# A gated delta-net stage: key chain rearranged, value pairs convolved from a copied slot, inverse's products four ticks later

## The chip, the cores and the metric

The kernel runs on one core of one Trainium2 chip. The metric is the device time of one execution in microseconds (us). Engines are named as in the profile: PE is TensorE (matmuls; PEld its weight loads), DVE is VectorE, ACT is ScalarE, POOL is GpSimd, SP is SyncE, whose queue issues the loads. SBUF is the core's main on-chip memory; PSUM holds the banks into which PE writes.

## What is computed

The reference is a trunk of two layers over 256 tokens of width 1024 (float32). Each layer is a feed-forward block, a mixer and a second feed-forward block, with RMS norms around each. The mixer of layer 0 is a short gated convolution; that of layer 1 is a gated delta-net, and the change lies in it alone. Cut to what matters:

```python
qkv = silu(causal_depthwise_conv(qkv, conv_w))          # width 4, on q, k and v
q = repeat(l2norm(q)); k = repeat(l2norm(k))            # 8 key heads for 16 value heads
beta = sigmoid(b)
g = -exp(a_log) * softplus(a + dt_bias)
# per head, in chunks of tokens:
a = strict(einsum(k_beta, k) * decay)
t_inv = triangular_solve(eye + a, eye)
u = t_inv @ v_beta; w = t_inv @ (k_beta * exp(g))
qk = causal(einsum(q, k) * decay)
# scan over chunks:
v_new = u - w @ state
o = (q * exp(g)) @ state + qk @ v_new
state = state * exp(g_last) + k_tail.T @ v_new
# out:
o = rms_norm(o) * norm_w * silu(z); y = o @ w_out
```

`l2norm(x)` is `x * rsqrt(sum(x * x) + EPS)`.

## The kernel before

The 256 tokens are two tiles of 128 (`NT` = 2, index t). A weight arrives as float32 by a DMA into a buffer `raw`, ACT rounds it to `whi` (L119) and DVE forms the rest `wlo` (L121, called a weight split below); each product of the reference is three matmuls (x with whi, the rest of x with whi, x with wlo). The heads are worked on in four groups (`NG` = 4, gi) of four value heads and two key heads (kh).

The function `gdn_proj` runs the products of the delta-net's input projection in this order: the first heads of queries and keys, the other queries and keys (`stat_group`, 24 products of 256 columns each, L278 to L280), the gate z of three groups (L221 to L225), the values of four groups, and the last z. The output projection follows (L323 to L325). Beside this main line run side chains, written as Python generators. A `Ticker` counts a tick for every twelve products of `stat_group`; `yield n` hands the program back to the main line for n ticks, so the numbers of ticks fix where in the program, and so where in each engine's queue, a side chain's step stands. Each engine works off its queue in that order and waits at an instruction until what it needs is there.

The side chains that matter here:

- `kq_chain` (L605): for each key head, PE transposes key and query into a bank `tp` (L618) and multiplies keys with keys and queries into a bank `pk` (L621). ACT copies the transposed key out (`ktok`, L624), copies the second token tile (`kq1`, L625), and takes four squares with a running sum (`junk`, L630), key and query of each token tile. At the end of a group, POOL adds EPS to the eight sums (L634), DVE takes the reciprocal (L636), POOL multiplies by beta (`dsc`, L639), and DVE scales the products by that and the decays (`KQ`, L645, eight steps). ACT copies the diagonal blocks of 32 x 32 into one tile (`blk`, L652, eight copies a group). POOL also forms `nk`, `eq` and `wt` for later use.
- `invert` (L667): it starts when `kq_chain` ends. DVE transposes the tile (L669), solves 31 steps (L677, L679), and transposes the inverse twice, into `Xd` (L681) and `Yd` (L683). POOL copies Yd's blocks into KQ (L689, 32 copies). `INV_WAIT` = 37 ticks after the start, in two halves, POOL fills blocks E from Xd (L699) and PE and ACT build the inverse of 128 x 128 from the blocks (L707 to L742).
- `v_pair` (L748): for two value heads, `conv` scales the bank on ACT (L584) and adds three taps on DVE for each head (L586), from the PSUM bank that the products were written to; silu follows on ACT (L573); `V_WAIT` = 4 ticks later PE transposes the result (L757) and ACT scales it out (`nv`, L759).
- `scan` waits for a group's values and inverse and then solves, updates the state and forms the outputs (L771 to L837); `z_chain` scales them with z (L846 to L855).

The banks that the side chains take come from a pool of four (`acc`), those of the main products and of the values' transposes from another of four (`mm`). Slots for tiles of 128 x 512 float32 come from one pool of 22 (`slab`); there are three buffers `raw`.

Of the kernel before, what the change touches and what calls it, by code (L numbers as in the profile page):

```python
# [7 lines left out]
F32 = mybir.dt.float32  # L8
F32R = mybir.dt.float32r
AF = mybir.ActivationFunctionType  # L10
ALU = mybir.AluOpType
PSUM = bass.MemoryType.PSUM

P = 128
T = 256
NT = 2
# [5 lines left out]
NG = 4  # L22
B32 = 32
EPS = 1e-6
# [6 lines left out]
NBIG = 8  # L31
NROW = 3
KQ_WAIT = 3
INV_WAIT = 37
V_WAIT = 4
SCAN_WAIT = 2
ORD = "00111222"
GORD = "00012222"
# [11 lines left out]
def trunk_kernel(ctx: ExitStack, tc: tile.TileContext, x, norm_g, w_gu, w_dn, sc_in, sc_cw, sc_out,  # L50
                 gdn_h0, gdn_h1, gdn_a0, gdn_a1, gdn_a2, gdn_v, gdn_z, gdn_cw, gdn_al, gdn_dt, gdn_nw, gdn_out, eye, upper, slower, out, stop=None):
    nc = tc.nc
    V, S, G, PE = nc.vector, nc.scalar, nc.gpsimd, nc.tensor
# [6 lines left out]
    sp = ctx.enter_context(tc.tile_pool(name="sp", bufs=2))  # L60
# [16 lines left out]
    phalf = const.tile([P, 4], F32, name="phalf")  # L77
# [49 lines left out]
    def slab(shape, dtype, name):  # L127
        return hp.tile(shape, dtype, name=name, tag="slab")
# [347 lines left out]
    def gdn_proj(xh, xl, mid):  # L476
# [102 lines left out]
        KQ = [[None] * NT for _ in range(NG)]  # L579
# [25 lines left out]
        def kq_chain():  # L605

            for gi in range(NG):
                ss = sp.tile([P, NT, 2, 2], F32, name="kss", bufs=2)
                k1 = slab([P, 2, 2, P], F32, "kq1")
                pkq = []  # L610
                for i in range(2):
                    kh = 2 * gi + i
                    while kq[kh] is None or tk.now < kq_time[kh] + KQ_WAIT:
                        yield 1
                    tp = side_bank().rearrange("p (t c) d -> p t c d", t=NT)
                    for t in range(NT):
                        for c in range(2):
                            PE.transpose(tp[:, t, c, :], kq[kh][:, c, t * P:(t + 1) * P], ident)  # L618
                    pk = side_bank().rearrange("p (t c) d -> p t c d", t=NT)
                    for t in range(NT):  # L620
                        PE.matmul(pk[:, t, :, :], lhsT=kq[kh][:, 0, t * P:(t + 1) * P],  # L621
                                  rhs=kq[kh][:, :, t * P:(t + 1) * P], start=True, stop=True)
                    pkq.append(pk)
                    S.activation(ktok[:, kh, :], tp[:, 0, 0, :], AF.Copy)  # L624
                    S.activation(k1[:, i, :, :], kq[kh][:, :, P:], AF.Copy)  # L625
                    kq1[kh] = k1[:, i, :, :]
                    for t in range(NT):
                        for c in range(2):
                            junk = sp.tile([P, 512], mybir.dt.bfloat16, name="junk", bufs=1)
                            S.activation(junk[:, 0:P], tp[:, t, c, :], AF.Square, accum_out=ss[:, t, c, i:i + 1])  # L630
                    yield 1
                while dec[1][gi] is None:
                    yield 1
                G.tensor_scalar(ss, ss, EPS, None, ALU.add)  # L634
                rk = sp.tile([P, NT, 2], F32, name="rk", bufs=2)
                V.reciprocal(rk, ss[:, :, 0, :])  # L636
                dd = small(f"dsc{gi}", 8).rearrange("p (t n) -> p t n", t=NT)
                for t in range(NT):
                    G.tensor_tensor(dd[:, t, :].rearrange("p (k v) -> p k v", k=2),  # L639
                                    beta[:, t, 4 * gi:4 * gi + 4].rearrange("p (k v) -> p k v", k=2),  # L640
                                    rk[:, t, :].unsqueeze(2).broadcast_to([P, 2, 2]), ALU.mult)
                for t in range(NT):
                    m = big([P, 4, 2, P], F32, "KQ")
                    for hv in range(4):
                        V.scalar_tensor_tensor(m[:, hv, :, :], pkq[hv // 2][:, t, :, :], dd[:, t, hv:hv + 1],  # L645
                                               bc(dec[t][gi][:, hv, :], 2), ALU.mult, ALU.mult)
                    KQ[gi][t] = m
                    for b in range(4):
                        r = slice(b * B32, (b + 1) * B32)
                        o = Ld[r, :, 8 * gi + t:8 * gi + t + 7:2].rearrange("p i v -> p v i")  # L650
                        i_ = m[r, :, 0, b * B32:(b + 1) * B32]
                        S.activation(o, i_, AF.Copy)  # L652
                n = small(f"nk{gi}", 4).rearrange("p (t n) -> p t n", t=NT)
                G.tensor_tensor(n, ss[:, :, 0, :], phalf.rearrange("p (t n) -> p t n", t=NT), ALU.pow)
                q = small(f"eq{gi}", 4).rearrange("p (t n) -> p t n", t=NT)
                G.tensor_scalar(q, ss[:, :, 1, :], 128.0 * EPS, None, ALU.mult)
                w = small(f"wt{gi}", 4)
                G.tensor_tensor(w, etail[:, 4 * gi:4 * gi + 4], dd[:, 0, :], ALU.mult)
                Dsc[gi], nk[gi], eq[gi], wt[gi] = dd, n, q, w
                yield 1  # L660
            tk.start(invert())


# [3 lines left out]
        def invert():  # L667
# [5 lines left out]
            for j in range(B32 - 1):  # L673
                n, m = B32 - 1 - j, j + 1
# [7 lines left out]
            Yd = row("blk").rearrange("p (a b) -> p a b", a=B32)  # L682
            V.transpose(Yd.rearrange("p h i -> p i h"), X)  # L683
            T1 = row("blk").rearrange("p (a b) -> p a b", a=B32)
            for gi in range(NG):
                for t in range(NT):
                    for b in range(4):
                        r = slice(b * B32, (b + 1) * B32)
                        G.tensor_copy(KQ[gi][t][r, :, 0, r], Yd[r, 8 * gi + t:8 * gi + t + 7:2, :])  # L689
            yield INV_WAIT  # L690
            for half in range(2):
                hs = slice(16 * half, 16 * half + 16)
                gis = (2 * half, 2 * half + 1)
                E = {}
                for gi in gis:
                    E[gi] = slab([P, 8, 64], F32, "E64")
                    for b in range(2):
                        r = slice(b * B32, (b + 1) * B32)
                        G.tensor_copy(E[gi][r, :, r], Xd[r, 8 * gi:8 * gi + 8, :])  # L699
                    G.memset(E[gi][0:B32, :, B32:], 0.0)  # L700
                pt = side_bank().rearrange("p a (b c) -> p (a b) c", c=B32)
                for x in range(16):
                    ht = 16 * half + x
# [42 lines left out]
        nv = [None] * NG  # L746

        def v_pair(gi, i, pt, tiles):  # L748
            vc = sp.tile([P, 2, T], F32, name="yb")
            for j in range(2):  # L750
                conv(vc[:, j, :], pt[:, j, :], 16 + 4 * gi + 2 * i + j)
            silu(vc, vc)
            yield V_WAIT
            tp = ps.tile([P, NT, 2, P], F32, name="mm")
            for t in range(NT):
                for j in range(2):
                    PE.transpose(tp[:, t, j, :], vc[:, j, t * P:(t + 1) * P], ident)  # L757
            for t in range(NT):
                S.activation(tiles[t][:, 2 * i:2 * i + 2, :], tp[:, t, :, :], AF.Copy,  # L759
                             scale=nk[gi][:, t, i:i + 1])  # L760
            if i == 1:
                nv[gi] = tiles
# [293 lines left out]
```

## Time and profile before

| what | us |
|---|---|
| median of three runs | 1131.45 (1130.69 to 1131.48) |
| profiled execution, its own time | 1128.42 |
| its span, from first to last instruction | 1126.5 |
| PE, DVE, ACT, POOL busy | 1100.2, 749.9, 651.8, 88.8 |
| mean granted TensorE clock | 0.995 |

A row of the timeline gives the start in the span, the duration, engine, line, operation, output and inputs by the program's names, the shape and the count; in brackets how long the engine stood idle before it and what it had waited for. Rows of groups give busy time and the mean in ns of one, then idle time before them. The view of one line gives the shortest, median and longest in ns. Names of buffers are given without their numbers.

### The profile page before, as it was taken

The numbers are of one execution on the slowest core, as the hardware profiler recorded it, in microseconds if no ns is written. First come the engines' busy times: TensorE is split into PE (matmuls) and PEld (weight loads), VectorE is DVE, ScalarE is ACT, GpSimd is POOL, SyncE is SP. The second block draws the span as 40 slices with busy tenths as digits, with TensorE's granted clock in tenths as the row PEclk, the third lists the DMA queues.
The fourth block names the chain that finished last, engine by engine and source line by source line (L and its number), as shares of the span: only waits on it lengthen the run. The fifth ranks groups of instructions, "written<-read, shape, count | busy, mean of one in ns | idle before, by whom it ended". The sixth has DMA issues, their size and how long they took to land.

```text
span 1126.5 us, 16842 instructions
## 1 busy us (share of the span) xinstructions
PE 1100.2 (98%) x6284; PEld 942.4 (84%) x6284; DVE 749.9 (67%) x1140; ACT 651.8 (58%) x1201; POOL 88.8 (8%) x167
## 2 busy tenths in 40 slices
PE   9999999999999999999999999889899999999997
PEld 6888887888788888788888877778899887888886
DVE  7776735687777663577765468768946557767543
ACT  6666535545556653556664358784587645666432
POOL 0100000000200000010000012110141212000000
PEclk9999999999999999999999999999999999999999
DMA  8755555656566565576555653327332355655552
GB/s 271 244 185 190 191 166 167 225 180 198 182 223 204 171 206 165 163 229 209 189 185 169 193 185 113 94 94 227 114 129 76 131 168 168 213 199 190 185 168 75
DMA packets 55955, 198.12 MB, mean 176 GB/s; under 512 B 6721, under 2 KB 7233, under 8 KB 55874
## 3 DMA queue, kind: packets, MB, share of 16 engines
q1 hardware_dynamic: 55728, 196.99, 54.2%
q8 instruction: 49, 0.80, 0.3%
q14 instruction: 32, 0.26, 0.1%
q10 hardware_dynamic: 146, 0.07, 0.0%
HBM read 195.99 MB, written 1.05 MB: 175 GB/s over the span
## 4 chain that ended last, share of the span: by engine, by line
PE 81%; DVE 7%; ACT 5%; DMA 3%; issue 2%; POOL 2%; SPq 0%; DVEq 0%; POOLq 0%; ACTq 0%
PE mm L298 27%; PE mm L301 14%; PE acc L324 7%; PE acc L325 7%; PE acc L323 7%; PE mm L221 3%; PE mm L222 3%; PE mm L225 3%; DVE wlo L121 2%; ACT whi L119 1%; ACT blk L652 1%; DVE kq L586 1%; PE mm L176 1%; ACT junk L147 1%; DMA raw<-in_w_gu 1%
## 5 line engine op out<-in xcount | busy, mean ns | idle before, releaser
L121 DVE TENSOR_TENSOR wlo<-raw,whi 128x1024 fp32r<-128x1024 f32 (+2 forms) x362 | 437.5, 1220 | 240.2 <-ACT whi L119 201.5
L119 ACT ACTIVATE whi<-raw 128x1024 fp32r<-128x1024 f32 (+2 forms) x362 | 376.1, 1051 | 224.3 <-PE acc L325 104.6
L298 PE MATMUL mm<-x,whi 128*128 128x512 f32 x1312 | 329.4, 393 | 0.0
L298 PEld LDWEIGHTS mm<-x,whi 128*128 128x128 f32 x1312 | 235.9, 189 | 42.4
L301 PEld LDWEIGHTS mm<-x,wlo 128*128 128x128 f32 x1312 | 179.0, 190 | 12.8
L301 PE MATMUL mm<-x,wlo 128*128 128x256 f32 x1312 | 182.9, 282 | 0.0
L323 PE MATMUL acc<-whi,hb 128*128 128x512 f32 x352 | 136.5, 388 | 0.0
L324 PE MATMUL acc<-wlo,hb 128*128 128x512 f32 x352 | 135.6, 385 | 0.3 <-DVE wlo L121 0.3
L325 PE MATMUL acc<-whi,hb 128*128 128x512 f32 x352 | 135.3, 385 | 0.0
L308 ACT ACTIVATE corr<-mm 128x256 f32<-128x256 f32 x164 | 61.2, 376 | 67.4 <-PE mm L301 65.6
L221 PE MATMUL mm<-whi,x 128*128 128x512 f32 (+1 forms) x240 | 94.4, 394 | 0.9 <-ACT x L178 0.7
L222 PE MATMUL mm<-wlo,x 128*128 128x512 f32 (+1 forms) x240 | 94.2, 393 | 0.7 <-DVE wlo L121 0.7
L225 PE MATMUL mm<-whi,x 128*128 128x512 f32 (+1 forms) x240 | 87.8, 389 | 0.2 <-DVE x L179 0.2
L324 PEld LDWEIGHTS acc<-wlo,hb 128*128 128x128 f32 x352 | 66.2, 188 | 13.8 <-DVE wlo L121 0.8
L323 PEld LDWEIGHTS acc<-whi,hb 128*128 128x128 f32 x352 | 66.2, 188 | 13.1
L325 PEld LDWEIGHTS acc<-whi,hb 128*128 128x128 f32 x352 | 66.1, 188 | 13.2
L154 POOL TENSOR_SCALAR rstd<-ss 128x1 f32<-128x1 f32 x24 | 12.3, 513 | 786.1 <-ACT junk L147 786.1
L278 PE MATMUL mm<-x,whi 128*128 128x256 f32 x200 | 59.7, 299 | 2.0 <-DVE kq L586 2.0
L279 PE MATMUL mm<-x,whi 128*128 128x256 f32 x200 | 58.4, 292 | 0.0
L280 PE MATMUL mm<-x,wlo 128*128 128x256 f32 x200 | 57.9, 289 | 0.0
L222 PEld LDWEIGHTS mm<-wlo,x 128*128 128x128 f32 x240 | 45.2, 188 | 11.2 <-DVE wlo L121 2.9
L221 PEld LDWEIGHTS mm<-whi,x 128*128 128x128 f32 x240 | 45.2, 188 | 11.1 <-ACT x L178 2.7
(216 smaller groups left out, 1238.3 us busy)
## 6 DMA issues: line engine op xcount, KB each, us to landing
raw<-in_w_gu SPq DMA_DIRECT2D x176, 512.0 KB, 4.2
raw<-in_w_dn SPq DMA_DIRECT2D x88, 512.0 KB, 3.6
raw<-in_sc_in SPq DMA_DIRECT2D x24, 512.0 KB, 4.1
raw<-in_gdn_z SPq DMA_DIRECT2D x16, 512.0 KB, 3.9
raw<-in_gdn_v SPq DMA_DIRECT2D x16, 512.0 KB, 4.2
raw<-in_gdn_out SPq DMA_DIRECT2D x16, 512.0 KB, 3.7
gamma<-in_norm_g SPq DMA_DIRECT2D x11, 512.0 KB, 5.4
raw<-in_gdn_a SPq DMA_DIRECT2D x9, 512.0 KB, 4.4
```

What stands on the lines that cost most here:

```text
L119: S.activation(hi[:, r], raw[:, r], AF.Copy)
L121: newest[0] = V.tensor_tensor(lo[:, r], raw[:, r], hi[:, r], ALU.subtract).ins
L221: PE.matmul(pt, lhsT=xh[:, t, k, :], rhs=hi, start=(k == 0), stop=False)
L222: PE.matmul(pt, lhsT=xh[:, t, k, :], rhs=lo, start=False, stop=False)
L225: PE.matmul(pt, lhsT=xl[:, t, j, :], rhs=part(j)[0], start=False, stop=(j == KD - 1))
L278: PE.matmul(ptile, lhsT=hi, rhs=h2, start=(k == 0), stop=False)
L298: PE.matmul(flat, lhsT=part(k, 0), rhs=xx[:, k].rearrange("p h t q -> p (h t q)"), start=(k == 0), stop=False)
L301: PE.matmul(flat[:, T:], lhsT=part(k, 1), rhs=xx[:, k, 0].rearrange("p t q -> p (t q)"), start=False, stop=(k == KD - 1))
L308: S.activation(c, pt[:, 1, :], AF.Copy)
L323: PE.matmul(o, lhsT=yh(c, t), rhs=hi[:, r], start=(c == 0), stop=False)
L324: PE.matmul(o, lhsT=yh(c, t), rhs=lo[:, r], start=False, stop=False)
L325: i = PE.matmul(o, lhsT=yl(c, t), rhs=hi[:, r], start=False, stop=(c == n - 1)).ins
```

## The change

`INV_WAIT` goes from 37 to 41 and `V_WAIT` becomes one number per group, (8, 8, 4, 4). In `kq_chain` the key squares come first, and all four squares stand ahead of the copies of `ktok` and `kq1`; the addition of EPS for the keys and `dsc` move from POOL to DVE, the addition for the queries becomes part of `eq`; and half of the diagonal copies move from ACT to POOL. In `invert` POOL's copies of Yd into KQ move behind the blocks E, in two halves. In `v_pair` the first two groups copy the bank to a slot (`vraw`) on ACT, and the conv reads that. After the change line numbers are one to nine higher.

```diff
-INV_WAIT = 37
-V_WAIT = 4
+INV_WAIT = 41
+V_WAIT = (8, 8, 4, 4)
+VRAW = 2
...
-                ss = sp.tile([P, NT, 2, 2], F32, name="kss", bufs=2)
+                ss = sp.tile([P, 2, NT, 2], F32, name="kss", bufs=2)
...
+                    for c in range(2):
+                        for t in range(NT):
+                            junk = sp.tile([P, 512], mybir.dt.bfloat16, name="junk", bufs=1)
+                            S.activation(junk[:, 0:P], tp[:, t, c, :], AF.Square, accum_out=ss[:, c, t, i:i + 1])
                     S.activation(ktok[:, kh, :], tp[:, 0, 0, :], AF.Copy)
                     S.activation(k1[:, i, :, :], kq[kh][:, :, P:], AF.Copy)
                     kq1[kh] = k1[:, i, :, :]
-                    for t in range(NT):
-                        for c in range(2):
-                            junk = sp.tile([P, 512], mybir.dt.bfloat16, name="junk", bufs=1)
-                            S.activation(junk[:, 0:P], tp[:, t, c, :], AF.Square, accum_out=ss[:, t, c, i:i + 1])
...
-                G.tensor_scalar(ss, ss, EPS, None, ALU.add)
+                V.tensor_scalar(ss[:, 0], ss[:, 0], EPS, None, ALU.add)
...
-                    G.tensor_tensor(dd[:, t, :].rearrange("p (k v) -> p k v", k=2),
+                    V.tensor_tensor(dd[:, t, :].rearrange("p (k v) -> p k v", k=2),
...
-                        S.activation(o, i_, AF.Copy)
+                        if b < 2:
+                            S.activation(o, i_, AF.Copy)
+                        else:
+                            G.tensor_copy(o, i_)
...
-                G.tensor_scalar(q, ss[:, :, 1, :], 128.0 * EPS, None, ALU.mult)
+                G.tensor_scalar(q, ss[:, 1], EPS, 128.0 * EPS, ALU.add, ALU.mult)
...
-            for gi in range(NG):
-                for t in range(NT):
-                    for b in range(4):
-                        r = slice(b * B32, (b + 1) * B32)
-                        G.tensor_copy(KQ[gi][t][r, :, 0, r], Yd[r, 8 * gi + t:8 * gi + t + 7:2, :])
             yield INV_WAIT
...
-                    G.memset(E[gi][0:B32, :, B32:], 0.0)
+                    placed = G.memset(E[gi][0:B32, :, B32:], 0.0).ins
+                for gi in gis:
+                    for t in range(NT):
+                        for b in range(4):
+                            r = slice(b * B32, (b + 1) * B32)
+                            with tc.issue_after(placed):
+                                G.tensor_copy(KQ[gi][t][r, :, 0, r], Yd[r, 8 * gi + t:8 * gi + t + 7:2, :])
...
+            if gi < VRAW:
+                raw = slab([P, 2, T], F32, "vraw")
+                S.activation(raw, pt, AF.Copy)
+                pt = raw
             vc = sp.tile([P, 2, T], F32, name="yb")
...
-            yield V_WAIT
+            yield V_WAIT[gi]
```

On DVE, at the end of the first group's keys, before (`kq` is a query or key under its conv, `rk` the reciprocal, `acc` the banks of products):

```order
L586 SCALAR_TENSOR_TENSOR kq_6753<-mm_6677,gcw_6224,kq_6753 128x255
L636 RECIPROCAL rk_6826<-kss_6549 128x4
L586 SCALAR_TENSOR_TENSOR kq_6753<-mm_6782,gcw_6224,kq_6753 128x255
L586 SCALAR_TENSOR_TENSOR kq_6753<-mm_6677,gcw_6224,kq_6753 128x254
L645 SCALAR_TENSOR_TENSOR KQ_6831<-acc_6740,dsc0_6828,dec_6622 128x256
L586 SCALAR_TENSOR_TENSOR kq_6753<-mm_6677,gcw_6224,kq_6753 128x253
L645 SCALAR_TENSOR_TENSOR KQ_6831<-acc_6740,dsc0_6828,dec_6622 128x256
```

And the same place after:

```order
L635 TENSOR_SCALAR kss_6549<-kss_6549 128x4
L637 RECIPROCAL rk_6826<-kss_6549 128x4
L640 TENSOR_TENSOR dsc0_6828<-beta_6233,rk_6826 128x4 x2
L646 SCALAR_TENSOR_TENSOR KQ_6831<-acc_6740,dsc0_6828,dec_6622 128x256 x2
L646 SCALAR_TENSOR_TENSOR KQ_6840<-acc_6740,dsc0_6828,dec_6627 128x256 x2
L646 SCALAR_TENSOR_TENSOR KQ_6831<-acc_6800,dsc0_6828,dec_6622 128x256
L587 SCALAR_TENSOR_TENSOR kq_6753<-mm_6677,gcw_6224,kq_6753 128x255
```

The two small steps of POOL now stand on DVE around the reciprocal, and the first five KQ steps stand ahead of the next key's conv taps.

On DVE, around the end of the inverse, before (`yb_7803` is the third value pair, `yb_7895` the fourth; `blk_7350` is Xd, `blk_7352` is Yd):

```order
L586 SCALAR_TENSOR_TENSOR yb_7803<-mm_7717,gcw_6224,yb_7803 128x253
L677 TENSOR_TENSOR sg_7344<-blk_7252,blk_7254 128x60
L121 TENSOR_TENSOR wlo_7870<-raw_7867,whi_7869 128x1024
L679 TENSOR_TENSOR blk_7254<-blk_7254,sg_7344 128x2x30
L586 SCALAR_TENSOR_TENSOR yb_7895<-mm_7783,gcw_6224,yb_7895 128x255
L677 TENSOR_TENSOR sg_7347<-blk_7252,blk_7254 128x31
L121 TENSOR_TENSOR wlo_8276<-raw_8273,whi_8275 128x1024
L679 TENSOR_TENSOR blk_7254<-blk_7254,sg_7347 128x31
L586 SCALAR_TENSOR_TENSOR yb_7895<-mm_7783,gcw_6224,yb_7895 128x254
L681 STREAM_TRANSPOSE blk_7350<-blk_7254 128x32x32
L683 STREAM_TRANSPOSE blk_7352<-blk_7254 128x32x32
L586 SCALAR_TENSOR_TENSOR yb_7895<-mm_7783,gcw_6224,yb_7895 128x253
```

After (`yb_7770` is the third value pair, `yb_7864` the fourth):

```order
L587 SCALAR_TENSOR_TENSOR yb_7770<-vraw_7768,gcw_6224,yb_7770 128x253
L681 TENSOR_TENSOR sg_7347<-blk_7252,blk_7254 128x31
L587 SCALAR_TENSOR_TENSOR yb_7770<-vraw_7768,gcw_6224,yb_7770 128x255
L683 TENSOR_TENSOR blk_7254<-blk_7254,sg_7347 128x31
L122 TENSOR_TENSOR wlo_8097<-raw_8094,whi_8096 128x1024
L685 STREAM_TRANSPOSE blk_7350<-blk_7254 128x32x32
L687 STREAM_TRANSPOSE blk_7352<-blk_7254 128x32x32
L587 SCALAR_TENSOR_TENSOR yb_7770<-vraw_7768,gcw_6224,yb_7770 128x254
L587 SCALAR_TENSOR_TENSOR yb_7864<-vraw_7862,gcw_6224,yb_7864 128x255
L587 SCALAR_TENSOR_TENSOR yb_7770<-vraw_7768,gcw_6224,yb_7770 128x253
```

Before, the third pair's last tap stood ahead of both transposes; now its last two taps stand behind them. On PE the third pair's transposes stand ahead of the inverse's first product in both kernels, 25 rows ahead of it.

On POOL, where the inverse's blocks are filled, before (`E64` are the blocks E):

```order
L699 COPY E64_7929<-blk_7350 32x8x32 x2
L699 COPY E64_7933<-blk_7350 32x8x32 x2
L700 MEMSET E64_7933 32x8x32
L699 COPY E64_8127<-blk_7350 32x8x32
L689 COPY KQ_6831<-blk_7352 32x4x32 x4
L689 COPY KQ_6840<-blk_7352 32x4x32 x4
L689 COPY KQ_6946<-blk_7352 32x4x32 x4
L689 COPY KQ_6955<-blk_7352 32x4x32 x4
L689 COPY KQ_7055<-blk_7352 32x4x32 x4
```

After:

```order
L698 COPY E64_7968<-blk_7350 32x8x32 x2
L699 MEMSET E64_7968 32x8x32
L705 COPY KQ_6831<-blk_7352 32x4x32 x4
L705 COPY KQ_6840<-blk_7352 32x4x32 x4
L705 COPY KQ_6946<-blk_7352 32x4x32 x4
L705 COPY KQ_6955<-blk_7352 32x4x32 x4
L698 COPY E64_8211<-blk_7350 32x8x32 x2
L699 MEMSET E64_8211 32x8x32
L698 COPY E64_8215<-blk_7350 32x8x32 x2
```

The second half's blocks E now stand behind sixteen of the copies into KQ, where before all but one of their steps stood behind all thirty-two.

On SP, two of the sixteen loads of the output weights move ahead of the two gamma loads (ten ahead and six behind, where it was eight and eight).

More of the change, by code (lines that the diff above doesn't have):

```diff
@@ L633, in kq_chain @@
                     yield 1
-                G.tensor_scalar(ss, ss, EPS, None, ALU.add)
+                V.tensor_scalar(ss[:, 0], ss[:, 0], EPS, None, ALU.add)
                 rk = sp.tile([P, NT, 2], F32, name="rk", bufs=2)
-                V.reciprocal(rk, ss[:, :, 0, :])
+                V.reciprocal(rk, ss[:, 0])
                 dd = small(f"dsc{gi}", 8).rearrange("p (t n) -> p t n", t=NT)
                 for t in range(NT):
-                    G.tensor_tensor(dd[:, t, :].rearrange("p (k v) -> p k v", k=2),
+                    V.tensor_tensor(dd[:, t, :].rearrange("p (k v) -> p k v", k=2),
                                     beta[:, t, 4 * gi:4 * gi + 4].rearrange("p (k v) -> p k v", k=2),
@@ L651, in kq_chain @@
                         i_ = m[r, :, 0, b * B32:(b + 1) * B32]
-                        S.activation(o, i_, AF.Copy)
+                        if b < 2:
+                            S.activation(o, i_, AF.Copy)
+                        else:
+                            G.tensor_copy(o, i_)
                 n = small(f"nk{gi}", 4).rearrange("p (t n) -> p t n", t=NT)
-                G.tensor_tensor(n, ss[:, :, 0, :], phalf.rearrange("p (t n) -> p t n", t=NT), ALU.pow)
+                G.tensor_tensor(n, ss[:, 0], phalf.rearrange("p (t n) -> p t n", t=NT), ALU.pow)
                 q = small(f"eq{gi}", 4).rearrange("p (t n) -> p t n", t=NT)
-                G.tensor_scalar(q, ss[:, :, 1, :], 128.0 * EPS, None, ALU.mult)
+                G.tensor_scalar(q, ss[:, 1], EPS, 128.0 * EPS, ALU.add, ALU.mult)
                 w = small(f"wt{gi}", 4)
```

## The prediction

> **What bounds the kernel now.** I began with the first part of the page, the busy time of each engine.
>
> ```profile
> PE 1100.2 (98%) x6284; PEld 942.4 (84%) x6284; DVE 749.9 (67%) x1140; ACT 651.8 (58%) x1201; POOL 88.8 (8%) x167
> ```
>
> TensorE (PE) is busy 98% of the span, so the kernel is bound by its matmuls, and the change adds and removes none. All that can change is the 26 us in which PE stands, and the time in which it runs slowly. Second I read the windows of ten microseconds through the stage that the diff touches. The columns are the window, PE, PEld, DVE, ACT and POOL busy with their instruction counts, the granted clock, the DMA share and GB/s.
>
> ```profile
> 720.00:730.00 10.00, 9.46 (x73) 8.70 (x72) 6.88 (x17) 9.54 (x35) 2.05 (x6) 1.00 0.11 42
> 730.00:740.00 10.00, 7.75 (x52) 6.94 (x51) 8.43 (x21) 8.79 (x24) 2.04 (x6) 1.00 0.29 106
> 740.00:750.00 10.00, 6.94 (x26) 5.48 (x25) 6.08 (x11) 8.55 (x30) 0.25 (x2) 0.83 0.36 110
> 790.00:800.00 10.00, 6.59 (x44) 6.39 (x43) 9.97 (x26) 6.57 (x10) 0.00 (x0) 0.83 0.22 63
> ```
>
> Two places lose time: 720 to 750, the key chain, where ScalarE (ACT) is the fullest helper, and 790 to 800, the first value heads, where VectorE (DVE) has no idle time at all. In both the granted clock falls to 0.83 in the worst window. Third I read who PE waits for between 715 and 835 us (total, times, longest).
>
> ```profile
> PE acc L618 <- ACT kq L573: 3.6, 2, 3.1
> PE mm L757 <- ACT yb L573: 3.4, 1, 3.4
> PE acc L621 <- DVE KQ L645: 1.7, 1, 1.7
> PE acc L618 <- ACT junk L630: 0.5, 2, 0.4
> PE acc L718 <- ACT blk L711: 0.4, 1, 0.4
> PE acc L707 <- DVE blk L681: 0.2, 1, 0.2
> ```
>
> The first, third and fourth rows are the key chain: 3.6 + 1.7 + 0.5 = 5.8 us. The second is the first value pair. The last two are the inverse's products. Last, the timeline of PE at the longest wait, which shows that a wait costs more than itself.
>
> ```profile
> 794.53 1.12 PE L757 MATMUL mm<-ident,yb 128*128 128x128 f32 x4 [3.41 <-ACT yb L573]
> ...
> 797.57 0.37 PE L279 MATMUL mm<-x,whi 128*128 128x256 f32 x1
> 797.78 0.28 PE L280 MATMUL mm<-x,wlo 128*128 128x256 f32 x1
> 797.90 0.28 PE L278 MATMUL mm<-x,whi 128*128 128x256 f32 x1
> ```
>
> Equal products start 0.21 us apart until 797.78 and 0.12 apart from then on. The slow spell lasts about 3.2 us from the restart, and 3.2 x (1 - 0.12/0.21) = 1.4 us is lost in it. The key chain's longest wait fills the other window of clock 0.83 (740 to 750, 3.06 us without PE), so I charge it the same 1.4; the 1.7 us wait lies in a window of clock 1.00, and nothing is charged. [...]
>
> **The key chain.** The chain per group was, in the rows of the first group on POOL and DVE:
>
> ```profile
> 717.26 0.66 POOL L634 TENSOR_SCALAR kss<-kss 128x8 f32<-128x8 f32 x1 [14.02 <-ACT junk L630]
> 718.00 1.05 POOL L654 TENSOR_TENSOR nk<-kss,phalf 128x4 f32<-128x4 f32 x1
> ...
> 719.45 0.35 POOL L639 TENSOR_TENSOR dsc<-beta,rk 128x4 f32<-128x4 f32 x2
> ...
> 719.68 0.48 DVE L645 SCALAR_TENSOR_TENSOR KQ<-acc,dsc,dec 128x256 f32<-128x256 f32 x1 [0.63 <-POOL dsc L639]
> ```
>
> From the first POOL step to the first KQ are 2.4 us, and nk, which the KQ step doesn't need, stands ahead of dsc for 1.05 of them. Now the addition, reciprocal and two dsc run on DVE; small DVE steps aren't all in this trace, and four of 0.2 us (POOL's dsc pair takes 0.35) make 0.8. That saves about 1.6 us a group. The key squares go to the front of ACT's list, where they pass two copies and four query squares. KQ then comes earlier, and the waits for KQ and for junk should go (2.2 us). What's late next is the silu of the queries, behind ACT's list. That list gets shorter by 16 of these 32 copies; this row prices a copy on ACT, and POOL's copies of the same shape (a row under the rivals) have a median of 0.29.
>
> ```profile
> L652 ACT ACTIVATE blk<-KQ 32x128 f32<-32x128 f32 x32 | 13.8, 430 | 2.3 <-DVE KQ L645 2.0
> ```
>
> So 16 x 0.43 = 6.9 us leave ACT and 16 x 0.29 = 4.6 go to POOL, which was 20% busy in these windows. Walking PE, ACT and DVE through the new order with these durations, I find the wait of 3.06 us down to 0.45, without a slow spell, and one new wait of 1.0 us for the keys' transposed copy (ktok), which now stands behind the four squares. Gain by the rows: 5.8 + 1.4 - 0.45 - 1.0 = 5.8 us. The same walk, read at the end of the last key product, gives 7.9, since a wait also delays the restart. I take 6.5; the bounds are 3.5 (two of the small margins of 0.1 to 0.3 us in the walk fail and cost another 2.3) and 8. The z products behind the key chain get no wait in the walk. The inverse, which starts when the last group's copies end, moves from 758.0 to about 749: 7.9 us from the chain, and about 1.1 because the last copies run on two engines.
>
> **The value pairs.** The first row is the first value product on PE; the second is the first pair's silu, which came late because its conv did, on a full DVE:
>
> ```profile
> 778.01 0.28 PE L278 MATMUL mm<-x,whi 128*128 128x256 f32 x1
> ...
> 793.84 0.63 ACT L573 ACTIVATE yb<-yb 128x512 f32<-128x512 f32 x1 [0.23 <-DVE yb L586]
> ```
>
> A tick is 12 products, 12 x 0.12 = 1.44 us. Before, the first transposes were due nine ticks in, at 778.0 + 13.0 = 791.0; they began at 794.53. Now they are due after 13 ticks, and the walk has the first product at 769.7: 769.7 + 18.7 = 788.4. Each next pair comes four ticks and its forerunner's transposes (0.44) later: 794.6 and 800.8. Conv and silu of the first two pairs end at 784.2 and 791.4 in the walk. So the wait of 3.4 goes with its slow spell: +4.8 us, with 3 to 4 us of cover left. The four bank copies cost ACT 4 x 0.63 = 2.5 us (the silu row has their shape), on an engine that has 3.4 us idle in the window of 790 to 800; they lie ahead of the conv, and that cover holds them.
>
> The inverse's products also move 4 ticks, and its 0.5 us of waits go, since its transposes end at about 800.2 and the products are due at 800.8 + 0.44 + 24 x 0.12 = 804.1. If that cover is gone it costs 0.2 to 0.5 again.
>
> **The new wait.** The third pair is the cost. Before, its conv was through before the inverse's two transposes of DVE; these rows are the inverse's first step, its two transposes, a tap of the fourth pair behind them, and the weight splits of 760 to 812:
>
> ```profile
> 758.02 1.25 DVE L669 STREAM_TRANSPOSE blk<-blk 128x1024 f32<-128x1024 f32 x1 [2.01 <-ACT blk L652]
> ...
> 809.80 2.20 DVE L681 STREAM_TRANSPOSE blk<-blk 128x1024 f32<-128x1024 f32 x1
> 811.89 1.96 DVE L683 STREAM_TRANSPOSE blk<-blk 128x1024 f32<-128x1024 f32 x1
> 813.69 0.41 DVE L586 SCALAR_TENSOR_TENSOR yb<-mm,gcw,yb 128x253 f32<-128x253 f32 x1
> ...
> L121 DVE TENSOR_TENSOR wlo<-raw,whi 128x1024 fp32r<-128x1024 f32 x18 | 21.9, 1217 | 2.0 <-ACT whi L119 1.7
> ```
>
> In the new order the last two of its six taps stand behind both transposes, with a tap of the fourth pair between. The inverse took 813.8 - 758.0 = 55.8 us on DVE from its first transposition to its last. One weight split (1.2) and four taps (4 x 0.41 = 1.6) fewer stand within now, so from 749 it ends at about 802.0. Three taps (1.2) and the silu (0.6) end at 803.8, while PE wants the pair at 800.8. (If the key chain yields less, both sides move together.) Waiting PE has the rest of the fifth pair's products and the inverse's products queued behind, and the scan follows those. That is 3.0 us; I take 2.9 and the slow spell of 1.4: -4.3. From below it costs almost nothing (the 2.0 us that DVE stood before splits close up, and the copies leave DVE sooner); from above 4.5 + 1.4 and 0.5 at the fifth pair, whose conv follows on DVE: -6.4.
>
> Behind this the order is the old one up to a block of products; the scan is 4 ticks later, its gamma loads two loads later. I put that at 0, with 1.5 either way. **Sum:** 6.5 + 4.8 + 0.5 - 4.3 = 7.5 us. The profiled run took 1128.42 us with a span of 1126.5, 1.9 outside it, and lies 3.0 under the median of 1131.45. I take the gain off the median: 1123.9 us.
>
> **Rivals.** *No third wait.* If DVE closes its gaps, the gain is 6.5 + 4.8 + 0.5 = 11.8: 1119.6. For it: the idle time of DVE. Against: the order, which holds whatever the speed.
>
> *The key chain hardly gains.* ACT was 95% busy from 720 to 730; if the queries' silu stays late and ktok's wait brings a slow spell, the key term is 2 and the gain 3.0: 1128.4.
>
> *POOL locked out (slower).* The value taps now read two SBUF tensors, and POOL copies 32 blocks beside them. This case shows what that does: taps out of SBUF beside POOL's selects, taps out of a bank, and POOL's copies beside weight splits.
>
> ```profile
> L586 DVE SCALAR_TENSOR_TENSOR kq<-mm,gcw,kq x27: 463/473/484, 705.4 to 743.6; 128x255 f32<-128x255 f32 x9, 128x254 f32<-128x254 f32 x9, 128x253 f32<-128x253 f32 x9
> L586 DVE SCALAR_TENSOR_TENSOR kq<-craw,gcw,kq x21: 472/475/861, 690.3 to 706.6; 128x255 f32<-128x255 f32 x7, 128x254 f32<-128x254 f32 x7, 128x253 f32<-128x253 f32 x7
> ...
> 812.07 1.72 POOL L699 COPY E<-blk 32x256 f32<-32x256 f32 x4 [58.84 <-DVE blk L681]
> ...
> L689 POOL COPY KQ<-blk x32: 283/287/1190, 815.4 to 827.6; 32x128 f32<-32x128 f32 x32
> ```
>
> A tap out of a bank never takes over 484 ns; out of SBUF it takes up to 861, and a copy up to 1190 instead of 287. The blocks E of a half are four copies, 1.72, and two memsets, by estimate from these copies 0.3 each: 2.3 us. So the copies begin at 800.2 + 2.3 = 802.5, and with the second half's E between, the last ends at 805 + 32 m for a mean of m each. PE wants it at 819.7 + 4.3 = 824. At the median of 0.29 they end at 814; from m = 0.59 PE waits, from m = 0.83 the gain of 7.5 is gone, and at 1.0, 837, the change is slower by 5.5: 1137. For it: three splits and seven taps fall beside the first half. Against: before, two of 32 copies were long. [...]
>
> **Chances.** The forecast 0.55 (own range 1121 to 1127), no third wait 0.23, key chain hardly gains 0.15, POOL locked out 0.07. The range of 1117 to 1130.5 takes in the upper bound of the key term on the good side (14 us of gain) and the lower bounds together on the other (3.5 + 4.8 + 0.5 - 6.4 - 1.5 = 0.9). A measurement of this kernel tells 0.2%, 2.3 us, from no change. The first two cases and a third of the third are faster by more: 0.83. Same: 0.10. Slower: 0.07.
>
> **What would show it.** Right: PE's waits for KQ and junk gone, the last wait for the queries under 1 us, the first value pair's wait gone, a new wait of about 3 us at the third value pair's transposes that ends with a silu behind the two transposes on DVE, and the inverse begun 8 to 9 us earlier. Wrong: more than 2 us of waits left from 720 to 750; no wait at the third pair; waits for POOL's copies in the inverse's last products; or new waits in the scan above 1.5 us.

## The result and the profile after

| kernel | median of 7 runs, us | lowest to highest |
|---|---|---|
| before | 1131.44 | 1130.69 to 1131.64 |
| after | 1123.13 | 1121.73 to 1129.65 |

The ratio is 0.9942, with a 95% interval of 0.9921 to 0.9962. That is 6.6 us by the ratio and 8.3 us by the medians, where 7.5 were forecast. The profiled execution of the changed kernel took 1122.99 us, its span was 1121.3.

The two profiles don't enter the stage at the same time, so all that follows is counted from the first transposes of keys on PE (704.00 before, 706.12 after). Three marks divide the stage: the first value product, the inverse's first step on DVE, and the start of the last three products of the output projection.

| from the first key transposes, us | before | after | forecast of the gain |
|---|---|---|---|
| inverse begins | 54.0 | 46.4 | 8 to 9 |
| first value product ("key part") | 74.0 | 66.5 | 6.5 (walk: 7.9) |
| from there to the stage's end ("value part") | 155.3 | 155.5 | 1.0 |

So the key part gave 7.5 us and the value part lost 0.2. Who PE waits for after 715 us, in the changed kernel (total, times, longest):

```profile
PE mm L766 <- ACT yb L574: 2.5, 1, 2.5
...
PE acc L622 <- ACT ktok L629: 1.0, 1, 1.0
PE acc L737 <- ACT E L727: 0.8, 1, 0.8
...
PE acc L723 <- ACT blk L716: 0.4, 1, 0.4
```

The rows for KQ, for the last query's silu and for the first value pair are gone. The wait of 1.0 for `ktok` is the one that was forecast, and the 2.5 is the third value pair. This is its chain: first the two last transposes of the inverse on DVE and the taps behind them, then the silu on ACT, then PE:

```profile
800.33 2.23 DVE L685 STREAM_TRANSPOSE blk<-blk 128x1024 f32<-128x1024 f32 x1
802.43 2.05 DVE L687 STREAM_TRANSPOSE blk<-blk 128x1024 f32<-128x1024 f32 x1
804.30 3.07 DVE L587 SCALAR_TENSOR_TENSOR yb<-vraw,gcw,yb 128x254 f32<-128x254 f32 x7
...
805.70 0.63 ACT L574 ACTIVATE yb<-yb 128x512 f32<-128x512 f32 x1 [0.75 <-DVE yb L587]
...
806.38 1.11 PE L766 MATMUL mm<-ident,yb 128*128 128x128 f32 x4 [2.45 <-ACT yb L574]
```

And POOL's copies of the inverse's blocks into KQ, 16 and 16, with what stands between:

```profile
805.40 9.59 POOL L705 COPY KQ<-blk 32x128 f32<-32x128 f32 x16
815.05 0.83 POOL L698 COPY E<-blk 32x256 f32<-32x256 f32 x2
...
816.28 2.74 POOL L698 COPY E<-blk 32x256 f32<-32x256 f32 x2
...
819.44 5.30 POOL L705 COPY KQ<-blk 32x128 f32<-32x128 f32 x16
```

The first half took 9.59 / 16 = 0.60 us a copy. Copy by copy, the six beside a tap out of a slot took 0.36 to 0.41 us, the four beside a weight split 1.17 to 1.31, and the other six, beside taps out of a bank or between DVE's steps, 0.29 or 0.30. The second half, beside a DVE that had no work but two taps out of a bank at its end, took 5.30 / 16 = 0.33 with the time between the copies. Over all 32 the mean is (9.59 + 5.30) / 32 = 0.47, under the 0.59 from which the prediction would have had PE wait, and PE didn't wait for them. The two copies into E at 815.05 stood beside taps out of a bank; those at 816.28 stood beside two weight splits and took more than three times as long.

The clock, in the windows of ten microseconds, is 0.83 in two places:

```profile
710.00:720.00 10.00, 10.00 (x71) 9.89 (x70) 8.12 (x20) 7.55 (x29) 1.41 (x4) 0.83 0.33 107
720.00:730.00 10.00, 9.03 (x66) 8.32 (x65) 8.37 (x20) 9.26 (x37) 3.93 (x7) 1.00 0.41 118
730.00:740.00 10.00, 10.00 (x73) 9.46 (x72) 9.37 (x25) 9.71 (x29) 5.66 (x9) 1.00 0.45 140
740.00:750.00 10.00, 10.00 (x47) 8.07 (x46) 8.88 (x21) 8.30 (x24) 3.86 (x7) 1.00 0.50 153
...
800.00:810.00 10.00, 7.55 (x51) 7.35 (x51) 10.00 (x13) 5.28 (x10) 6.79 (x14) 0.83 0.21 59
```

From 730 to 750 PE is full now, where it was busy 7.75 and 6.94. The largest loss sits at 800 to 810.

### The profile page after: what moved, and what is told of

Its sections match the earlier page's. It is cut to its first block, busy times and chain, and to the rows that moved or that the text cites. A ratio compares the mean times of both kernels' runs of the same rounds, so it can differ in the third digit from the quotient of the medians.

```text
span 1121.3 us, 16866 instructions
## 1 busy us (share of the span) xinstructions
PE 1100.0 (98%) x6284; PEld 942.7 (84%) x6284; DVE 753.1 (67%) x1152; ACT 647.5 (58%) x1189; POOL 98.1 (9%) x171
## 3 DMA queue, kind: packets, MB, share of 16 engines
q1 hardware_dynamic: 55728, 196.99, 53.9%
## 5 line engine op out<-in xcount | busy, mean ns | idle before, releaser
L120 ACT ACTIVATE whi<-raw 128x1024 fp32r<-128x1024 f32 (+2 forms) x362 | 376.2, 1051 | 228.8 <-PE acc L326 104.1
L325 PEld LDWEIGHTS acc<-wlo,hb 128*128 128x128 f32 x352 | 66.2, 188 | 13.7 <-DVE wlo L122 0.8
L324 PEld LDWEIGHTS acc<-whi,hb 128*128 128x128 f32 x352 | 66.2, 188 | 13.4 <-ACT hb L473 0.2
L279 PE MATMUL mm<-x,whi 128*128 128x256 f32 x200 | 59.6, 298 | 2.0 <-DVE kq L587 2.0
```

The lines of the kernel that those rows point to most:

```text
L120: S.activation(hi[:, r], raw[:, r], AF.Copy)
L279: PE.matmul(ptile, lhsT=hi, rhs=h2, start=(k == 0), stop=False)
L324: PE.matmul(o, lhsT=yh(c, t), rhs=hi[:, r], start=(c == 0), stop=False)
L325: PE.matmul(o, lhsT=yh(c, t), rhs=lo[:, r], start=False, stop=False)
```

## The experiments

Theory to test, as the prediction had it: the parts add up, 6.5 us from the key chain and 1.0 from the rest. Each ratio is to the kernel before on the same chip. "Key chain alone" is the kernel before with the whole new `kq_chain` (squares first, small steps on DVE, half of the copies on POOL) and nothing else.

**One part each.** `e1_key_only` is the key chain alone.

> The key chain's part alone, on the kernel before. The prediction's theory: the parts are independent, and the key chain is worth 6 to 7.5 us; the first value pair keeps its wait of about 3.4 us with its slow spell. Time 1124 to 1125.5, ratio about 0.994. Rival (the key chain hardly gains, the gain came with the value pairs): 1 to 3 us, ratio 0.997 to 0.999.

Measured: 1120.17 us against 1130.74, ratio 0.9909 (0.9891 to 0.9928). The key chain alone gives more than the whole change: its five runs (1118.96 to 1121.18) all lie under the changed kernel's seven (from 1121.73) and its six of a later repetition (from 1121.74). PE's waits and the first value pair in it:

```profile
PE mm L760 <- ACT yb L573: 1.9, 2, 1.6
PE acc L621 <- ACT ktok L628: 1.0, 1, 1.0
...
786.37 0.66 PE L760 MATMUL mm<-ident,yb 128*128 128x128 f32 x4 [1.58 <-ACT yb L573]
```

With four ticks and no slots, the wait of 3.41 us has become 1.58, without a slow spell behind it. The inverse leads the first value product by 20.1 us, as before (20.0). But from its first step to about the pair's silu DVE does 13 weight splits where it did 14, and stands 1.0 us before them where it stood 2.0 (these rows are of before, 758 to 794 us, and of the key chain alone, 751.5 to 787):

```profile
L121 DVE TENSOR_TENSOR wlo<-raw,whi 128x1024 fp32r<-128x1024 f32 x14 | 17.0, 1218 | 2.0 <-ACT whi L119 1.7
```

```profile
L121 DVE TENSOR_TENSOR wlo<-raw,whi 128x1024 fp32r<-128x1024 f32 x13 | 15.8, 1218 | 1.0 <-ACT whi L119 1.0
```

That makes 2.2 us, and the pair's wait is 1.8 shorter. The parts don't add: what the later transposes were to remove, the key chain had mostly removed.

`e2_value_only` is the changed kernel with the old `kq_chain`.

> All of the change but the key chain's part. The prediction's theory: the first pair's 4.8 us and 0.5 us at the inverse go, a wait of 2.5 to 3 us with a slow spell of 1.4 comes at the third value pair: gain 1 to 1.5 us, ratio about 0.999. Rival (no third wait without the earlier inverse): gain 5 us, ratio 0.9955. Rival (the key chain hardly gains, so this part carries the 8 us): ratio 0.993 to 0.994.

Measured: 1137.18, ratio 1.0061 (1.0040 to 1.0083): slower, which no theory had. Its waits:

```profile
PE mm L763 <- ACT yb L574: 3.9, 1, 3.9
...
PE acc L720 <- ACT blk L713: 1.6, 2, 1.2
PE mm L223 <- DVE wlo L122: 1.2, 1, 1.2
```

The first pair's wait is gone, the third pair's is 3.9, and two more follow. From the first value product on, the waits are 7.4 us where before had 4.1, and behind them PE loses 6.8 us to a slower clock where before lost 1.7.

**The third pair's wait.** `e3_third_first` is the changed kernel with

```diff
+            yield INV_TR
             Xd = row("blk").rearrange("p (a b) -> p a b", a=B32)
             V.transpose(Xd.rearrange("p h c -> p c h"), X.rearrange("p i c -> p c i"))
...
-            yield INV_WAIT
+            yield INV_WAIT - INV_TR
```

and `INV_TR = 33`, which puts five of the third pair's taps ahead of the first transpose and the sixth between the two.

> The changed kernel with the inverse's two last transposes created 33 ticks later, so that five taps of the third value pair stand ahead of the first of them and the sixth ahead of the second. The prediction's theory: the third pair's wait of 2.5 us falls to 0.3 or less and its slow spell of about 1.4 goes, nothing takes its place: 3.5 to 4 us less than the changed kernel, about 1119.3, ratio 0.9907. Rival (VectorE is the bound of this stretch, so that the wait moves to the fifth pair and to the blocks E of the inverse): at most 1 us less, ratio 0.9935.

Measured: 1122.97, ratio 0.9935 (0.9917 to 0.9953), as the rival had it. The third pair no longer waits, and the inverse's next step does:

```profile
811.82 0.47 ACT L586 ACTIVATE yb<-mm,gcw 128x256 f32<-128x256 f32 x1 [1.16 <-DVE yb L588]
812.32 1.20 ACT L718 ACTIVATE blk<-acc 32x512 f32<-32x512 f32 x2
...
812.96 0.31 PE L725 MATMUL acc<-blk 32*32 32x32 f32 x2 [3.59 <-ACT blk L718]
```

The copy that PE waits for stands on ACT behind a scaling that waits for DVE's taps. DVE was busy 9.90 and 10.00 of 10 us in the windows 790 to 800 and 800 to 810, so here a step moved ahead of another only changed who waits.

`e4_no_vraw` is the changed kernel with `VRAW = 0`.

> The changed kernel without the copies from bank to slot: all convs read the bank, all waits as changed. Theory that the copies only cost ScalarE 2.5 us that is hidden: within 1 us of the changed kernel, the third pair's wait stays at 2 to 3 us. Rival (the slots are what lets the transposes come eight ticks later, since a bank held until the conv's end makes the products wait): new waits of TensorE for a bank behind a conv, 2 us or more, ratio 0.996 or worse.

Measured: 1121.26, ratio 0.9927 (0.9907 to 0.9948), no different from the changed kernel's. The slots bring nothing that can be told. Without them the third pair's wait is gone (its last tap stands ahead of the transposes), a wait of 0.9 for a bank comes (L279 behind `nv`), and 2.2 at the inverse's second step (L723).

**Which edit costs.** `f1_key_vals` is the key chain alone with the new `v_pair`; `f2_key_inv` is it with the new `invert` and 41 ticks.

> The key chain's part with the change to the value pairs (8, 8, 4, 4 ticks and the slots), the inverse as before. Theory: with the key chain alone the first pair's wait is down to 1.6 us, so the later transposes have 1.9 us to win, and VectorE's two long transposes take it back: a wait of about 1.3 us at the inverse's first product and about 1 at the third pair; 1119.5 to 1121, ratio 0.990 to 0.9915. Rival (the later transposes and slots alone cost the 3 us that lie between the key chain alone and the whole change): 1123, ratio 0.9935.

> The key chain's part with the change to the inverse (41 ticks, POOL's copies behind the blocks E), the value pairs as before. Theory: nothing waits for the inverse in the kernel with the key chain alone, so four ticks more bring nothing, and they cost nothing as the scan has work beside it: within 1 us of it, ratio 0.990 to 0.992. Rival (the scan four ticks later lays its serial steps open near the end, or POOL's locked copies are late for the last products): 2 to 3 us more, ratio 0.993 to 0.9935.

Measured: 1120.64 us, ratio 0.9932 (0.9910 to 0.9954), and 1122.60 us, ratio 0.9936 (0.9922 to 0.9951). `f2_key_inv` lies nearer to its rival, 3 us above the key chain alone. `f1_key_vals` is not decided: its median lies in the theory's range, but two of its nine runs took 1126.2 and 1128.4, and by the ratio it lies with the rival. Both intervals overlap with that of the key chain alone. Of the two waits that the theory of `f1_key_vals` named, the one at the inverse's first product is there (1.5); the other came at the inverse's second step (1.7) and not at the third pair. In `f2_key_inv` the scan's L784 waits 1.2 us for DVE and a block E 0.6.

**What in the key chain it is.** From the key chain alone, one edit undone each: all copies to `blk` on ACT (`f3_key_actblk`), EPS and `dsc` on POOL (`g1_key_poolsmall`), the four squares behind the two copies and in the old order (`g2_key_oldsq`).

```diff
-                        if b < 2:
-                            S.activation(o, i_, AF.Copy)
-                        else:
-                            G.tensor_copy(o, i_)
+                        S.activation(o, i_, AF.Copy)
```

> The key chain's part with all 32 diagonal copies on ScalarE as before. Theory: the 6.9 us that left ScalarE's list are what made the last query's silu early: its wait of 2.5 to 3 us with the slow spell of 1.4 comes back, and the inverse starts 1 us later: 4 to 5 us more than the key chain alone, 1124.5, ratio 0.995. Rival (the gain is in the short chain from squares to KQ alone): less than 1.5 us more, ratio 0.992 or better.

Measured: 1127.91, ratio 0.9981 (0.9969 to 0.9993), 8 us of the 10 lost. The theory's wait came back (3.5), another of 1.9 with it, and the first pair's of 3.9. That pair bears out the reading of the weight splits above. The inverse leads the first value product by 20.9 us here. But from its first step to the pair's last tap pass 37.2 us, with 13 splits and 3.3 us of standing before them; in the kernel before it was 35.7, with 13 and 1.7, and in the key chain alone 34.0, with 12 and 1.0. PE's waits:

```profile
PE mm L757 <- ACT yb L573: 3.9, 1, 3.9
PE acc L618 <- ACT kq L573: 3.5, 1, 3.5
...
PE acc L618 <- ACT ktok L628: 1.9, 1, 1.9
```

```diff
-                V.tensor_scalar(ss[:, 0], ss[:, 0], EPS, None, ALU.add)
+                G.tensor_scalar(ss[:, 0], ss[:, 0], EPS, None, ALU.add)
...
-                    V.tensor_tensor(dd[:, t, :].rearrange("p (k v) -> p k v", k=2),
+                    G.tensor_tensor(dd[:, t, :].rearrange("p (k v) -> p k v", k=2),
```

> The key chain's part with the addition of EPS and the two multiplications by beta left on POOL. Theory: KQ comes about 1 us later in each group, a wait for KQ or its banks comes back and the inverse starts 1 to 2 us later, which the first value pair waits for: 2 to 3.5 us more than the key chain alone, ratio 0.9930 to 0.994. Rival (only the copies that left ScalarE count): at most 1 us more, ratio 0.991 to 0.992.

Measured: 1122.35, ratio 0.9942 (0.9928 to 0.9956), at the slow end of what the theory had: the inverse begins 1.8 us later (46.7 from the key transposes), leads the first value product by 18.7 instead of 20.1, and the first value pair waits 3.8.

> The key chain's part with the four squares behind the two copies and in the old order. Theory: the squares' place moves the start of the short chain by the time of two copies and two squares, about 1 us a group, and the bank's last reader stays as late: 0 to 1 us more than the key chain alone, ratio 0.991 to 0.992. Rival (the squares' place is a third of the gain): 2.5 to 3.5 us more, ratio 0.9935.

Measured: 1130.05, ratio 1.0006 (0.9992 to 1.0020): the whole gain lost, more than the rival had. The key part is still 66.2 long. But the inverse begins at 51.6 instead of 44.9. The last group's second key is transposed 3.0 us later, and from there to the addition of EPS pass 5.3 us instead of 1.6, as two weight roundings of 1.06 us now stand between its squares on ACT. The inverse's first transposed result (Xd) is ready 37.1 us after the first value product instead of 30.5. The value part is 162.1 instead of 152.5, and 8.5 us of it are lost to a slower clock, where the key chain alone lost none. Its longest wait is for POOL, and 6.8 of the 8.5 are lost right behind it:

```profile
811.95 15.11 POOL L692 COPY KQ<-blk 32x128 f32<-32x128 f32 x32
...
827.90 1.97 PE L735 MATMUL acc<-E,KQ 64*64 64x64 f32 x16 [2.25 <-POOL E L703]
```

The block E of the second half stands behind all 32 copies into KQ in this old order. So the copies' move, which the prediction gave no value of its own, should take away a wait where the inverse is late. This kernel with the new order of the copies was not run.

**A better version.** `f4_key_ktok_v6` is the key chain alone with

```diff
                             S.activation(junk[:, 0:P], tp[:, t, c, :], AF.Square, accum_out=ss[:, c, t, i:i + 1])
+                        if c == 0:
+                            S.activation(ktok[:, kh, :], tp[:, 0, 0, :], AF.Copy)
```

and 6 ticks for the first group's values.

> The key chain's part with the copy of ktok between the key squares and the query squares, and 6 ticks instead of 4 for the first group's values, without slots. Theory: the wait of 1.0 us for ktok and the 1.9 us at the first two value pairs go and nothing takes their place: 1117.3, ratio 0.988. Rival (as with the third pair in the run before, a wait removed here comes back behind: at KQ, as its squares come later, or at the inverse's products): within 1 us of the key chain alone, ratio 0.990 to 0.992.

Measured: 1118.30, ratio 0.9901 (0.9885 to 0.9917), 0.9 us under the key chain alone, not told from it. It is the fastest kernel here, 12 us under the one before by the medians. The wait for `ktok` didn't go: it is 1.0 us long as before and now ends with a square.

```profile
PE acc L621 <- ACT junk L627: 1.0, 1, 1.0
```

So PE doesn't wait for `ktok` there but, as far as this shows, for the bank, whichever step of ACT reads it last. That takes away the reason which the prediction gave for its 1.0 us.

`g3_v65_inv38` goes one step on, with 6 and 5 ticks for two groups and 38 for the inverse.

> The key chain's part with ktok between the squares, 6 and 5 ticks for the first two groups' values, 38 for the inverse, no slots. Theory (a wait goes for good where VectorE has reached the instruction by the new time): of the third pair's 1.3 us and the inverse's 0.8 and 0.5 about 1.5 to 2 go, and 1116.5 is reached, ratio 0.9885. Rival (VectorE is the bound of the stretch, so each tick is given back behind): within 0.5 us of 6, 4, 4, 4 and 37 ticks, ratio 0.990.

Measured: 1128.51, ratio 1.0000 (0.9985 to 1.0015). Neither theory had that. With the value pairs' waits ahead of it gone, PE came 4.7 us early for the block E behind POOL's 32 copies, and then ran slowly. POOL, PE, and the windows:

```profile
805.76 13.17 POOL L693 COPY KQ<-blk 32x128 f32<-32x128 f32 x32 [0.17 <-DVE blk L687]
...
819.75 1.97 PE L736 MATMUL acc<-E,KQ 64*64 64x64 f32 x16 [4.73 <-POOL E L704]
...
810.00:820.00 10.00, 5.27 (x79) 4.77 (x72) 3.65 (x7) 4.59 (x13) 8.86 (x28) 0.67 0.36 109
820.00:830.00 10.00, 10.00 (x121) 9.54 (x122) 1.23 (x1) 4.30 (x9) 1.92 (x6) 0.50 0.17 55
830.00:840.00 10.00, 10.00 (x176) 9.07 (x171) 3.66 (x5) 7.45 (x17) 0.00 (x0) 0.81 0.27 68
```

At the median of 0.29 us a copy that the kernel before had, the 32 would by estimate have taken 9.3 us and not 13.2, so both their place and their slowness make this wait. The key chain alone with `f4`'s ticks and the new order of POOL's copies was not run.

`g4_after_again` is the changed kernel on the chip of the last three.

> The changed kernel once more, beside the others on the same chip. Theory: 1122.5 to 1123.5, ratio about 0.994, 2.5 to 3 us slower than the key chain alone. Rival (the difference between the two lies in the chip): ratio 0.991 to 0.992.

Measured: 1123.25, ratio 0.9951 (0.9934 to 0.9967). Its interval lies above that of the key chain alone (0.9891 to 0.9928); the two were timed on different chips, each against the kernel before.

**All profiles in one table.** Waits are PE's from 715 to 880 us; the clock's loss is ten times one minus the granted clock, summed over the windows from 700 to 880; the rest is the stage less both. Each row is one execution.

| kernel | key part | inverse begins | value part | stage | waits | clock's loss | rest |
|---|---|---|---|---|---|---|---|
| before | 74.0 | 54.0 | 155.3 | 229.3 | 10.0 | 5.1 | 214.2 |
| after | 66.5 | 46.4 | 155.5 | 222.0 | 4.9 | 3.4 | 213.7 |
| after again | 66.5 | 46.4 | 158.7 | 225.2 | 6.6 | 5.1 | 213.5 |
| key chain alone | 65.0 | 44.9 | 152.5 | 217.6 | 3.3 | 0.0 | 214.3 |
| without it | 73.9 | 53.9 | 162.0 | 235.8 | 12.1 | 10.3 | 213.4 |
| third pair first | 66.5 | 46.4 | 156.2 | 222.8 | 5.1 | 5.1 | 212.6 |
| no slots | 65.0 | 44.9 | 153.6 | 218.6 | 4.3 | 0.0 | 214.3 |
| key chain, new values | 66.5 | 46.4 | 155.6 | 222.2 | 4.2 | 5.1 | 212.9 |
| key chain, new inverse | 66.7 | 46.6 | 155.0 | 221.7 | 5.3 | 1.7 | 214.7 |
| copies on ACT | 72.3 | 51.4 | 156.5 | 228.8 | 9.3 | 6.8 | 212.7 |
| small steps on POOL | 65.5 | 46.7 | 155.9 | 221.3 | 5.2 | 3.4 | 212.7 |
| old squares | 66.2 | 51.6 | 162.1 | 228.3 | 6.1 | 8.5 | 213.7 |
| 6, 4 ticks | 64.8 | 44.7 | 152.8 | 217.6 | 3.6 | 0.0 | 214.0 |
| 6, 5 and 38 | 66.2 | 46.1 | 165.3 | 231.5 | 8.9 | 12.0 | 210.6 |

The rest is the same within some 2 us but for the last row, where 3 us of half rate fell into the wait of 4.73, so that 1.5 us are counted in both columns. So nearly all that differs between these kernels is PE's waits and the clock behind them. The 1.5 us by which the key part differs between 65.0 and 66.5 is one step of the clock at the stage's start (see the end), and the profile before has that step too. So of the 9.0 us by which the key part is shorter in the key chain alone, 1.5 are a matter of where that step fell; the comparison of the times above doesn't rest on it.

## Why the prediction was right, point by point

The total was right, and so were the places that it named in the changed kernel. That the total came so near was in part luck: the key part gave 1.0 us more than was put, the value part 1.2 less. The key part measured 7.5 us where 6.5 were put; the walk's 7.9 was nearer. The inverse began 7.6 us earlier, a little short of the 8 to 9 that were put. The wait for KQ, those for junk and the last query's silu went, and a wait of 1.0 came at the first step named (0.97 measured), though for the bank and not for `ktok`. The first value pair's wait went. The new wait came at the third pair, 2.45 us where 2.9 were put, behind the two transposes as described, and with a slow spell.

Three terms were wrong in size or in what they were put down to.

- **The 4.8 us of the first value pair.** The prediction gave them to the eight ticks. The key chain alone shows that the wait would have been 1.6 without a slow spell: some 3 us of the 4.8 belonged to the key chain, behind which DVE had a split less to do and stood less ahead of the conv. The prediction took the old wait as given once the inverse and the values moved together. So the eight ticks had about 1.9 us of waits to win, and the change as a whole has 2.45 and a spell in their place; beside the new key chain, the rest of the change loses 3 us by the medians and 3.7 by the ratios.
- **The 0.5 us at the inverse.** 0.4 stayed, at L723, and 0.8 came at L737: -0.7 in the place of +0.5. "If that cover is gone it costs 0.2 to 0.5" left out the step at L737, whose copy (L727) stands on ACT behind the values' silu.
- **The 1.4 us of a slow spell.** It was charged after each long wait and after no other. A spell is no fixed price of a wait (below). The prediction counted two before and one after, and the profiles have three and two: a spell at the stage's start, seen before as a clock of 0.95 and 0.88 in the windows from 700 to 720, was left out on both sides. That it cancelled was luck.

*POOL locked out*, the slower rival, didn't decide here. No run shows a lock; what the runs show is slower copies and taps. A copy took 0.60 us in the first half against 0.33 in the second, most of all beside weight splits (1.17 to 1.31 against 0.29). The taps out of a slot took up to 644 ns in the changed kernel, where none of the taps out of a bank took over 485 in either profile (the prediction had 484). In the old order of the copies, PE did wait behind them where it came early (4.73 us in `g3`) or the inverse late (2.25 in `g2`). *No third wait* fell with the first profile, and *the key chain hardly gains* with the key part's 7.5 us.

## What to carry to other kernels

Run each part of a change alone before believing that the parts add: here one part carried more than the whole. On a stretch where a helper engine never idles (here DVE, busy 9.90 and 10.00 of 10 us from 790 to 810 in `e3_third_first`), count when it begins and how much stands in its list: moving a step there only changed who waits (2.45 us at the third pair became 3.59 at the inverse's second step). And copy work off the fullest list first: sixteen small copies moved from ScalarE to GpSimd were worth 8 us of 1130, and the place of four squares as much or more. Either of them undone alone lost most of the gain, so these amounts don't add either.

## What the runs showed of the hardware

The clock's loss comes in steps: 1.7, 3.4, 5.1, 6.8, 8.5, 10.3 and 12.0 us are one to seven times 1.7, which is 3.4 us at half the rate (before, the window from 709.0 to 712.4 alone has a clock of 0.50). Whether a step comes isn't set by the wait's length alone. All fourteen profiles hold the same wait of about 2.0 us for a query's conv early in the stage; eight have one step behind it and six have none. These are the wait and the window behind it in the key chain alone, to be held against the 0.83 of the changed kernel's window above, behind a wait of 1.98:

```profile
710.13 0.39 PE L278 MATMUL mm<-x,whi 128*128 128x256 f32 x1 [1.98 <-DVE kq L586]
...
710.00:720.00 10.00, 9.87 (x77) 9.61 (x78) 9.59 (x24) 8.84 (x31) 2.21 (x5) 1.00 0.35 107
```

What tells the two apart, as far as these profiles show it, is where the wait falls. In these profiles the slow spells start whole multiples of 3.413 us apart. Before, they start at 709.02, 746.56, 794.35 and 1125.44; the last is 416.43 us, or 122 times 3.413, behind the first, the others 11 and 25 times. In the changed kernel they start at 710.75, 806.32 and 1120.35, 28 and 120 times behind the first. To a tenth of a us it is the same in `f1_key_vals` (709.8 and 808.8, 29 times) and in `g2_key_oldsq` (786.8 and 827.8, 12 times). In seven of the eight (the place of the wait in `f2_key_inv` isn't known) 1.90 us of the early wait or more lie in the last 3.41 us before the spell that follows it; in the changed kernel the wait lasts from 707.65 to 709.63. In three of the six, a later spell in the stage, counted back by whole multiples of 3.413 us, gives a time inside the wait: 708.3 in `g2` from 786.8 (the wait lasts from 706.78 to 708.75), 708.5 in `g1` from 787.0 (707.67 to 709.63) and 707.7 in `f3` from 724.8 (706.10 to 708.07). So there about 1.6 us of it at most lie on one side of that time. In the other three no spell falls into the stage, so it isn't shown for them. Nor do the runs show why the spells start at such distances.

Longer waits differ in the same way. Waits of 2.4 us (without the key chain) and 2.6 (after again) had no step behind them, and the times counted from the spells of their profiles, 748.6 and 804.0, fall inside them; the 2.45 of the changed kernel had one; and all eight waits of 3.06 us and more had at least one. A wait of 2.2 us (no slots) had none, in a stage without a spell. Waits of 1.7 us, with no such time inside them, had a step behind them in two profiles (without the key chain, after again) and none in another (before). The standing alone doesn't explain every spell: three (808.8 in `f1_key_vals`, 827.1 without the key chain, 816.7 in `g3_v65_inv38`) began where PE had stood about 0.3, 0.3 and 0.5 of the 3.41 us before, and in each of them it ran the inverse's products of 32 x 32 or 64 x 64 for another 1.1 us or so. A step can also be followed by others without a further wait, as in `g3_v65_inv38`, where one spell from 816.7 on, behind the one wait of 4.73, lasted 17.1 us. What keeps the clock down there stays open.

The spread of the times goes with the clock: the changed kernel's fastest and slowest run lie 7.9 us apart, 0.7%, and their mean clocks, 0.996 and 0.989, are 0.7% apart too.
